# Sixteen start addresses for the split FFN weights of a two-layer decoder trunk

## The chip, the cores and the metric

The kernel runs on one core of one Trainium2 chip. The metric is the device time of one execution in microseconds; the kernel before takes 1004.91 us (median of 2 runs, 1004.67 to 1005.15).

## The reference

A trunk of two layers over one sequence of 256 tokens and 1024 features, in float32. Each layer has an FFN, an attention, and a second FFN, each ahead of it a root-mean-square norm that is scaled and shifted by vectors computed from `c`. So there are four FFNs:

```python
def swiglu(h, w_in, w_out):
    g, u = jnp.split(h @ w_in, 2, axis=-1)
    return (jax.nn.silu(g) * u) @ w_out
...
for layer in range(DEPTH):
    ...
    x = x + 0.5 * g1[:, None, :] * swiglu(h, ffn_w_in[layer, 0], ffn_w_out[layer, 0])
    ...
    x = x + g2[:, None, :] * mix
    h = modulate(rms_norm(x, norm_g[layer, 2]), sh3, sc3)
    x = x + 0.5 * g3[:, None, :] * swiglu(h, ffn_w_in[layer, 1], ffn_w_out[layer, 1])
return rms_norm(x, final_g)
```

The hidden width is 2816 (`FF`), so `w_in` is 1024 x 5632 and `w_out` is 2816 x 1024.

## The kernel before

Activations are kept transposed: 128 features on the partitions, the 256 tokens along each partition. A weight block of 128 x 128 is the stationary operand of a matmul (it is loaded into TensorE first, the profile's PEld), and 256 columns of activations are its moving operand. To keep float32 accuracy with a faster matmul type, every operand is split in two: a high part in the type fp32r and the rest, a low part. `mm3` (line 398) then makes three matmuls of each block: high weights by high activations, low weights by high activations, high weights by low activations. In the trace the weights' parts are `wh` and `wl`. The activations' parts are `HH` and `HL` (the normed input of a stage, rows of 320 words for each group of 128 features) in an FFN's first half of work, and `hidh` and `hidl` (the hidden units, tiles of 512 words) in its second.

All weights come in one fixed order, `stream`, cut in pieces of at most 1024 words per partition (`pieces`). For each piece there is a DMA from HBM into a buffer `raw`, a cast by ScalarE into a buffer `wh` (`cp_part`, line 288), and a subtraction by VectorE into a buffer `wl` (`sub_part`, line 298). There are 6 buffers `raw`, 6 `wh` and 5 `wl`, used in turn.

A buffer `wh` or `wl` is `WB` = 1088 words long, 64 more than a piece. 1088 words are 4352 bytes, or 17 x 256, so all eleven buffers start at the same address mod 256, which is 64 in the built program. `HH`, `HL`, `hidh` and `hidl`, and every block of 256 columns in them, start at 0 mod 256. So the distance "activations less weights, mod 256" is 192 for every such matmul. A dictionary `shift` moves the start of a piece's `wh` and `wl` inside its buffer by so many words. Before, it holds 16 words (64 bytes, distance 128) for six pieces: one at the second group of `win` of the FFN (0, 1), two at the first group of (1, 0), three at the second group of (1, 1):

```python
for (l, i), j, count in ((0, 1), 1, 1), ((1, 0), 0, 2), ((1, 1), 1, 3):
    first = next(...)
    shift.update({first + p: 16 for p in range(count)})
...
wh = wp.tile([P, WB], F32R, tag="wh", name="wh")[:, shift.get(u, 0):]
wl = wp.tile([P, WB], F32R, tag="wl", name="wl", bufs=NLO)[:, shift.get(u, 0):]
```

An FFN (`ffn(l, i, ...)`, line 532) has two stages. In the first, eleven groups of 256 hidden units are made from `win`: tiles `pg` and `pu`, 96 matmuls of 256 columns for a group, 24 for each piece of 1024 words. In the FFN (0, 0) the first four groups come from an own array `win0` (tiles `pf`) and seven from `win`. In (0, 1) and (1, 1) the first group is made ahead of the norm, with two further columns, so that its matmuls have 258 columns (tiles `lg`, `lu`). In the second stage, eight blocks of 128 output features are made from `wout` (tiles `po`), 66 matmuls each. Between the FFNs (0, 0) and (0, 1) stands the first attention (`wqk`, `wv`, `wo`; tiles `pqk`, `pv`, `pw`), between (0, 1) and (1, 0) the shared keys and values (`wkk`, `wkv`; tiles `lp`, `pk`, `pzf`, `pv`), between (1, 0) and (1, 1) the second attention.

The order on each engine is that in which the program is written. A small planner (`InOrder`, `bg`, `fill_act`, `fill_dve`) decides while the program is built where casts, subtractions and the dot products for `c` (`ada`) stand between the rest; its costs know sizes of operands, not addresses. Every instruction is issued through line 103, so the rows of the profile all name L103 and are told apart by their tiles.

Of the kernel before, what the change touches and what calls it, by code (L numbers as in the profile page):

```python
# [25 lines left out]
NG = FF // 256  # L26
# [5 lines left out]
K0 = 4  # L32
# [10 lines left out]
FRONT = 0  # L43
TAIL = 4
PLAN = [1, 1, 1, 1, 2, 1, 2, 3, 1, 3]
PACE = [0.62, 0.74, 0.62, 0.38, 0.76, 0, 0.74]
NRAW = 6
NLO = 5
# [59 lines left out]
def trunk(ctx, tc, a, out):  # L108
# [127 lines left out]
    def win0_of(l, i):  # L236
        return 0 if (l, i) == (0, 0) else 2 * (NG - K0) + 2 * NG * (2 * l + i - 1)

    def add_ffn(l, i):
        if (l, i) == (0, 0):  # L240
# [18 lines left out]
    pieces = [(src, c0, min(step, ncols - c0), c0 + step >= ncols)  # L259
              for src, ncols, step in stream for c0 in range(0, ncols, step)]  # L260

    shift = {}
    for (l, i), j, count in ((0, 1), 1, 1), ((1, 0), 0, 2), ((1, 1), 1, 3):
        first = next(p for p, v in enumerate(pieces) if v[0].tensor is a["win"].tensor
                     and v[0].offset == a["win"][win0_of(l, i) + 2 * j].offset)
        shift.update({first + p: 16 for p in range(count)})
    raws, his, los = [], [], []
    taken = [0]
    begun = [0]
# [228 lines left out]
    def late_pairs(src, dsts, m, then):  # L498

        pb = []

        def out(i):
            c = late_cols(pb[i])
            for b in range(2):
                t = kp.tile([P, S], F32, tag="sq", name="lt")
                dve.tensor_tensor(t, pb[i][b][:, :S], r, op=ALU.mult)
                act.activation(dsts[i][:, b * S:(b + 1) * S], t, AF.Identity, bias=c[:, b:b + 1])

        for i in range(2):
            banks = [mmbank(f"lp{i}{b}") for b in range(2)]
            pb.append(banks)
            blk = take(src)
            for k in range(NC):
                for b in range(2):
                    mm3(banks[b][:, :SX], blk(k * 256 + b * P), hx[k], k == 0, k == NC - 1)
                if i == 0:
                    if k == 2:
                        r = rstd_of(then)  # L520
                        mh = MakeH(r, m)
                else:
                    if k == 0:
                        out(0)
                    mh.go()
        mh.go(9 - mh.k)
        out(1)
        mode[0] = "run"
        return r
# [292 lines left out]

    pace[0] = PACE[0]
    ffn(0, 0, rstd, ((0, 1), (0, 0)), ((0, 4), (0, 3)))
# [173 lines left out]

    pace[0] = PACE[1]
    op = attention_a()  # L1000
    op.finish((0, 5), ((0, 7), (0, 6)))
    pace[0] = PACE[2]
    ffn(0, 1, "late", ((0, 7), (0, 6)), (("kv", 1), ("kv", 0)), at=3)
# [9 lines left out]
    for i in range(2):  # L1013
# [7 lines left out]
        fgs += [(fgh[:, k], fgl[:, k]) for k in range(4)]  # L1021
    pace[0] = PACE[3]
    rstd = late_pairs("wkk", kT, (("kv", 1), ("kv", 0)), AF.Exp)
# [46 lines left out]

    pace[0] = PACE[4]
    ffn(1, 0, "ready", None, ((1, 4), (1, 3)))

    def attention_b():
# [88 lines left out]
        def step(n):  # L1163
            for _ in range(n):
                next(fill, None)

        step(FRONT)
        for t in range(BH + 3):
            n0, n1 = PLAN[2 * (t // 4):2 * (t // 4) + 2]
            step(n0)  # L1170
# [15 lines left out]

    pace[0] = PACE[5]
    op = attention_b()
# [134 lines left out]
```

## Time and profile before

| | |
|---|---|
| median of 2 runs | 1004.91 us |
| the profiled execution, its own time | 1006.43 us |
| its span, first to last instruction | 1004.7 us |
| TensorE busy (matmuls) | 979.0 us, 97% |
| TensorE weight loads | 941.3 us, 94% |
| VectorE busy | 820.9 us, 82% |
| ScalarE busy | 563.3 us, 56% |
| mean granted TensorE clock | 0.997 |

The span is the time from the first to the last instruction of the program; the profiled execution's own time is 1.7 us longer. Matmuls overlap in a pipeline, so a matmul that is shown with 276 ns doesn't cost 276 ns: what it costs is the time from its start to the next one's start.

### The profile page before, as it was taken

What the parts mean: (1) busy time and instruction counts of PE and PEld (TensorE: products, weight loads), DVE (VectorE), ACT (ScalarE), POOL (GpSimd) and SP (SyncE); (2) the same over time, 40 slices, a digit from 0 to 9 for tenths busy, and PEclk for the clock granted to TensorE, in tenths of its full rate; (3) what the DMA queues carried; (4) which work ended last, traced back from release to release, by engine and by line L of the source; (5) the groups of instructions that cost most, each with busy time, mean ns of one, the idle gap of its engine ahead of it and who ended that gap; (6) DMA issues with size and microseconds to landing.
All of it is one profiled execution on the core that took longest, in us unless ns stands there. A gap on an engine that the chain in (4) does not pass through costs nothing.

```text
span 1004.7 us, 20432 instructions
## 1 busy us (share of the span) xinstructions
PE 979.0 (97%) x8076; PEld 941.3 (94%) x8076; DVE 820.9 (82%) x1379; ACT 563.3 (56%) x922; POOL 37.1 (4%) x64
## 2 busy tenths in 40 slices
PE   5999999999999999999999999999999999999996
PEld 4999999988989999999988999999987799999996
DVE  6989979889889998888698988889897787555553
ACT  5465545575877645455476455454575576454552
POOL 0000100000111000000000000000011010000000
PEclk9999999999999999999999999999999999999998
DMA  8988999958765899888757999989744337665661
GB/s 347 414 333 285 334 364 345 348 199 320 264 211 196 272 403 356 288 283 308 275 191 304 363 339 327 331 296 336 245 147 122 107 125 236 198 193 153 172 183 43
DMA packets 68131, 265.08 MB, mean 264 GB/s; under 512 B 7961, under 2 KB 8113, under 8 KB 57922
## 3 DMA queue, kind: packets, MB, share of 16 engines
q1 hardware_dynamic: 65810, 258.31, 73.3%
q0 software_dynamic: 1792, 4.81, 1.8%
q8 instruction: 63, 1.03, 0.4%
q10 hardware_dynamic: 432, 0.64, 0.2%
q14 instruction: 34, 0.28, 0.1%
HBM read 262.66 MB, written 2.65 MB: 264 GB/s over the span
## 4 chain that ended last, share of the span: by engine, by line
PE 92%; DVE 3%; ACT 2%; issue 1%; DMA 1%; SPq 0%; POOL 0%; DVEq 0%; POOLq 0%; ACTq 0%
PE po L103 24%; PE pg L103 21%; PE pu L103 21%; PE pf L103 5%; PE pv L103 4%; PE pw L103 4%; PE lp L103 2%; PE pqk L103 2%; PE pk L103 1%; PE pob L103 1%; PE lg L103 1%; PE lu L103 1%; PE sb L103 1%; DVE wl L103 1%; DMA ada<-in_ada 1%
## 5 line engine op out<-in xcount | busy, mean ns | idle before, releaser
L103 DVE TENSOR_TENSOR wl<-raw,wh 128x1024 fp32r<-128x1024 f32 (+1 forms) x368 | 401.3, 1104 | 92.8 <-issue 24.7
L103 ACT CAST wh<-raw 128x1024 fp32r<-128x1024 f32 (+1 forms) x368 | 349.3, 958 | 208.7 <-PE pu L103 96.5
L103 DVE CUSTOM_DVE_ANT_0 ada<-ada,cact,vecs 128x1024 f32<-128x1024 f32 x160 | 203.3, 1278 | 0.0
L103 PE MATMUL po<-hidl,wh 128*128 128x256 f32 x704 | 194.3, 276 | 0.0
L103 PE MATMUL po<-hidh,wh 128*128 128x256 f32 x704 | 194.3, 276 | 0.0
L103 PE MATMUL po<-hidh,wl 128*128 128x256 f32 x704 | 194.3, 276 | 0.0
L103 PE MATMUL pg<-HH,wh 128*128 128x256 f32 x608 | 168.1, 276 | 0.0
L103 PE MATMUL pg<-HH,wl 128*128 128x256 f32 x608 | 168.0, 276 | 0.0
L103 PE MATMUL pg<-HL,wh 128*128 128x256 f32 x608 | 168.0, 276 | 0.0
L103 PE MATMUL pu<-HH,wl 128*128 128x256 f32 x608 | 167.9, 276 | 0.0
L103 PE MATMUL pu<-HH,wh 128*128 128x256 f32 x608 | 167.9, 276 | 0.0
L103 PE MATMUL pu<-HL,wh 128*128 128x256 f32 x608 | 167.9, 276 | 0.0
L103 PEld LDWEIGHTS po<-hidh,wh 128*128 128x128 f32 x704 | 132.2, 188 | 0.0
L103 PEld LDWEIGHTS po<-hidh,wl 128*128 128x128 f32 x704 | 132.2, 188 | 0.0
L103 PEld LDWEIGHTS po<-hidl,wh 128*128 128x128 f32 x704 | 132.2, 188 | 0.0
L103 PEld LDWEIGHTS pg<-HH,wh 128*128 128x128 f32 x608 | 114.2, 188 | 0.7 <-issue 0.6
L103 PEld LDWEIGHTS pg<-HH,wl 128*128 128x128 f32 x608 | 114.2, 188 | 0.0
L103 PEld LDWEIGHTS pu<-HL,wh 128*128 128x128 f32 x608 | 114.2, 188 | 0.0
L103 PEld LDWEIGHTS pu<-HH,wl 128*128 128x128 f32 x608 | 114.1, 188 | 0.0
L103 PEld LDWEIGHTS pg<-HL,wh 128*128 128x128 f32 x608 | 114.1, 188 | 0.0
L103 PEld LDWEIGHTS pu<-HH,wh 128*128 128x128 f32 x608 | 114.1, 188 | 0.0
L103 ACT ACTIVATE HH<-ht,modall 128x256 fp32r<-128x256 f32 x56 | 27.8, 507 | 40.4 <-DVE ht L103 38.9
(204 smaller groups left out, 1604.7 us busy)
## 6 DMA issues: line engine op xcount, KB each, us to landing
raw<-in_win SPq DMA_DIRECT2D x176, 512.0 KB, 5.9
ada<-in_ada SPq DMA_DIRECT2D x79, 1024.0 KB, 7.4
raw<-in_wout SPq DMA_DIRECT2D x64, 384.0 KB, 4.9
raw<-in_wout SPq DMA_DIRECT2D x64, 320.0 KB, 4.3
raw<-in_wqk SPq DMA_DIRECT2D x16, 512.0 KB, 5.0
raw<-in_wo SPq DMA_DIRECT2D x16, 512.0 KB, 5.2
raw<-in_wv SPq DMA_DIRECT2D x8, 512.0 KB, 7.4
raw<-in_wkk SPq DMA_DIRECT2D x8, 512.0 KB, 8.1
```

The source lines that it names most:

```text
L103: return self.tc.keep_in_program_order(f(*args, **kw))
```

## The change

The dictionary `shift` is filled by another rule. A table `PHASES` gives a distance for each of sixteen halves of a stage: eight for `win` (two halves for each FFN, in the FFNs' order) and eight for `wout`. Every piece of `win` and of `wout` gets its start moved so that the distance from the activations has that value mod 256. The 16-word shifts of the six pieces are gone. `win0` and the weights of the attentions and of the shared keys and values keep the distance 192.

```diff
+PHASES = dict(win=(208, 224, 32, 48, 112, 144, 200, 184), wout=(240, 16, 80, 96, 160, 176, 168, 216))
...
     shift = {}
-    for (l, i), j, count in ((0, 1), 1, 1), ((1, 0), 0, 2), ((1, 1), 1, 3):
-        first = next(p for p, v in enumerate(pieces) if v[0].tensor is a["win"].tensor
-                     and v[0].offset == a["win"][win0_of(l, i) + 2 * j].offset)
-        shift.update({first + p: 16 for p in range(count)})
+    for name, at in PHASES.items():
+        ps = [p for p, v in enumerate(pieces) if v[0].tensor is a[name].tensor]
+        for p in ps:
+            u = (pieces[p][0].offset - a[name].offset) // math.prod(a[name].shape[1:])
+            if name == "wout":
+                q = divmod(u, 8)[0]
+            else:
+                f = 0 if u < win0_of(0, 1) else 1 + (u - win0_of(0, 1)) // (2 * NG)
+                b = win0_of(f // 2, f % 2)
+                q = 2 * f + (u - b >= (NG - K0 if f == 0 else NG))
+            shift[p] = (192 - at[q]) % 256 // 4
```

In the order of the program, with the number of matmuls by half:

| FFN | `win`, first and second half | `wout`, first and second half |
|---|---|---|
| (0, 0) | 208 (336), 224 (336) | 240 (264), 16 (264) |
| (0, 1) | 32 (96 of 258 columns, 432), 48 (528) | 80 (264), 96 (264) |
| (1, 0) | 112 (528), 144 (528) | 160 (264), 176 (264) |
| (1, 1) | 200 (96 of 258 columns, 432), 184 (528) | 168 (264), 216 (264) |

No instruction is added, taken away or moved: on every engine the same operations on the same tiles stand in the same order. What differs is the start of `wh` and `wl` inside their buffers.

## The prediction

> **What bounds the kernel now.** The page comes first: the engines' busy time, the clock, and the chain that ended last.
>
> ```profile
> span 1004.7 us, 20432 instructions
> PE 979.0 (97%) x8076; PEld 941.3 (94%) x8076; DVE 820.9 (82%) x1379; ACT 563.3 (56%) x922; POOL 37.1 (4%) x64
> PEclk9999999999999999999999999999999999999998
> PE 92%; DVE 3%; ACT 2%; issue 1%; DMA 1%; SPq 0%; POOL 0%; DVEq 0%; POOLq 0%; ACTq 0%
> ```
>
> TensorE is busy throughout at the full clock, and 92% of the chain is its own matmuls. The other engines count only where they make it wait. So the question is what one matmul costs in the FFNs. A table of the busy time in chosen windows shows it: us, then for each engine its busy time and the number of instructions. The windows are the FFNs after the first: groups 1 to 10 of (0, 1), then `wout`; (1, 0); groups 1 to 10 of (1, 1).
>
> ```profile
> 323.80:432.70 108.90, 108.90 (x962) 108.90 (x962) 98.84 (x134) 56.36 (x72) 0.00 (x0) 1.00 0.88 314
> 432.70:492.70 60.00, 60.00 (x530) 59.80 (x528) 51.14 (x80) 32.41 (x48) 1.93 (x4) 1.00 0.90 315
> 547.20:667.20 120.00, 120.00 (x1058) 119.96 (x1057) 106.32 (x141) 59.34 (x70) 0.00 (x0) 1.00 0.91 326
> 825.40:934.60 109.20, 109.20 (x962) 109.20 (x961) 66.12 (x74) 56.13 (x71) 0.00 (x0) 1.00 0.60 186
> ```
>
> TensorE never stops there: 960 matmuls in 108.9 us are 113.4 ns each, 528 in 60.0 us are 113.6 (the counts take in two that overlap the edges). Nothing in these stages waits for VectorE, ScalarE or a DMA; VectorE is nearly full in the first three (98.84 of 108.90) and half idle in the last, and the cost of a matmul is the same. What ends last is the beat of load and matmul itself.
>
> **What the beat depends on.** The change touches nothing but addresses, so I looked for stretches that run without a stop at another beat. Five windows: the three pieces at distance 128 (72 matmuls by the code); the piece-sized stretch behind them at 192 (72); `pzf`, whose weights start at 0 mod 256 (distance 0, 24 matmuls); the group `pk3` at 192 (48); and `lg`/`lu` at 192 with 258 columns (39).
>
> ```profile
> 825.44:833.98 8.54, 8.54 (x74) 8.54 (x73) 8.20 (x15) 6.36 (x14) 0.00 (x0) 1.00 0.43 123
> 835.36:843.52 8.16, 8.16 (x74) 8.16 (x73) 7.47 (x9) 5.64 (x7) 0.00 (x0) 1.00 0.77 244
> 514.71:517.59 2.88, 2.88 (x27) 2.88 (x26) 2.43 (x4) 2.88 (x5) 0.00 (x0) 1.00 0.15 51
> 517.58:523.24 5.66, 5.66 (x50) 5.66 (x49) 5.66 (x7) 5.57 (x9) 0.00 (x0) 1.00 0.81 250
> 319.05:323.76 4.71, 4.71 (x42) 4.71 (x40) 4.35 (x11) 3.16 (x6) 0.00 (x0) 1.00 0.65 226
> ```
>
> Divided by the matmuls that start in them: 118.6 ns at distance 128, 113.3 at 192, 120.0 at 0, 117.9 at 192 in `pk3`, and 120.8 with 258 columns. Two facts follow. The distance bears on the beat: where it goes from 128 back to 192 in the middle of group 1 of (0, 1), with nothing else changed, the starts in order of time close up within three matmuls.
>
> ```profile
> 325.90 0.28 PE L103 MATMUL pu<-HH,wh 128*128 128x256 f32 x1
> 326.02 0.28 PE L103 MATMUL pu<-HH,wl 128*128 128x256 f32 x1
> 326.14 0.28 PE L103 MATMUL pu<-HL,wh 128*128 128x256 f32 x1
> 326.25 0.28 PE L103 MATMUL pu<-HH,wh 128*128 128x256 f32 x1
> ...
> 326.95 0.28 PE L103 MATMUL pg<-HH,wh 128*128 128x256 f32 x1
> 327.07 0.28 PE L103 MATMUL pg<-HH,wl 128*128 128x256 f32 x1
> 327.18 0.28 PE L103 MATMUL pg<-HL,wh 128*128 128x256 f32 x1
> 327.29 0.28 PE L103 MATMUL pu<-HH,wh 128*128 128x256 f32 x1
> ```
>
> Four starts before the seam span 0.35 us, four behind it 0.34. And the distance alone doesn't settle it: `pk3` runs at 117.9 at the good distance. So at 192 there are two steady ways to run, a good beat and one off it, and the one in which a stage starts it keeps.
>
> **The good beat is the floor.** A row for each kind of matmul gives the shortest, the middle and the longest duration; off the beat they are longer (the second pair: `pk` off the beat, `pzf`).
>
> ```profile
> L103 PE MATMUL po<-hidh,wh x704: 276/276/276, 139.9 to 994.1; 128*128 128x256 f32 x176
> L103 PE MATMUL pg<-HH,wh x608: 276/276/385, 62.8 to 933.6; 128*128 128x256 f32 x152
> ...
> L103 PE MATMUL pk<-HL,wh 128*128 128x256 f32 x16 | 4.5, 281 | 0.0
> ...
> L103 PE MATMUL pzf<-HH,fgh 128*128 128x256 f32 x8 | 2.3, 283 | 0.0
> ```
>
> The middle one is the shortest one: of the 1312 in the first two rows, at distances 192 and 128 and after every kind of disturbance, none is shorter than one on the good beat. What speaks for a lower floor are matmuls of another type (float32, 128 columns), which take less:
>
> ```profile
> L103 PE MATMUL po<-va,wt x48: 271/275/275, 245.5 to 298.2; 128*128 128x128 f32 x48
> L103 PE MATMUL po<-tri,on x16: 272/272/273, 253.8 to 303.0; 128*128 128x128 f32 x16
> ```
>
> [...]
>
> **The change part by part.** (1) *Taken away:* the six pieces at distance 128. 6 x 24 = 144 matmuls at 118.6 - 113.3 = 5.3 ns over the floor: at most 0.8 us to gain. The 192 matmuls of 258 columns (`lg`, `lu`) are 7.5 ns over it; at 32 and 200 they could gain up to 1.4 us or lose nothing that I can price, and I take 0. So the most that the floor leaves is 2.2 us.
>
> (2) *Added:* new distances for 2 x 336 + 6 x 528 + 8 x 264 = 5952 matmuls, 5760 without those of 258 columns. Off the beat each costs 4.6 ns (`pk3`) to 6.7 (`pzf`) more; I take 5.3, as at 128, which is the case nearest to a weight piece that starts elsewhere in an FFN. All 5760 off it: 5760 x 5.3 = 30.5 us, by the ends 26.5 to 38.6. None: 0.
>
> How many? No run here shows any of the sixteen. Of the three distances that the trace has, 192 can hold the beat and 0 and 128 don't, in 24 and 144 matmuls. Six halves' distances lie within 24 bytes of 192 (168, 176, 184, 200, 208, 216): 336 + 432 + 528 + 3 x 264 = 2088 matmuls. For them I take the nearest row, 192, with one way of two: half off the beat, 1044. The other ten (3672 matmuls) lie nearer to 0, to 128, or to 64, of which no row of an FFN tells: I take the count of three, two thirds off, 2448. Together 3492 x 5.3 = 18.5 us.
>
> (3) *The writers.* ScalarE and VectorE write at other starts. The row for 1024 words with a shift of 64 bytes, and the one behind it without:
>
> ```profile
> L103 DVE TENSOR_TENSOR wl<-raw,wh 128x1024 fp32r<-128x1024 f32 x4 | 4.9, 1217 | 0.0
> ...
> L103 DVE TENSOR_TENSOR wl<-raw,wh 128x1024 fp32r<-128x1024 f32 x5 | 5.9, 1216 | 0.0
> ```
>
> 1 ns. A start 8 bytes off a multiple of 16 (168, 184, 200, 216) isn't shown. What hides a slower write is VectorE's idle time: in 547.20:667.20, 13.7 us over 44 pieces, some 0.3 us for each write of 1.2; above a quarter more it would come on the path. I take 0. The DMAs land in `raw`, whose addresses stay.
>
> (4) *Seams.* Fifteen changes of distance without a stop, three matmuls each by the starts above: under 0.3 us.
>
> Sum: 18.5 - 0.8 = +17.7 us, against a profiled execution of 1006.43 us (span 1004.7). That execution lies 0.15% over the median of the runs, so I add the difference to the median: 1004.9 + 17.7 = 1022.6, say **1022 us**.
>
> [...]
>
> **The rivals.** *A, the forecast:* some halves keep the beat, some don't, 1009 to 1030. Chance 0.58.
>
> *B, not slower:* the good beat, once entered, holds at every distance but a few, as it holds at 192 through each seam from `pg` to `po`, where tiles and strides change and the beat doesn't; (0, 0) enters it from `pf` at 192, and every later half takes it over. Its place are the seams, its price 0, its gain 0.8 us: 1004.1. It decides if 0 and 128 are special, as multiples of 128. Against it: three stages at 128 in a row never fell into the beat. Chance 0.14, with what lies up to 1009.
>
> *C, nearly all lose it:* the beat needs a start on a multiple of 64, as every operand that the trace shows has, and none of the sixteen is one; a row of weights then costs what two columns more cost the 258-column matmuls, 7.5 ns. 5952 x 7.5 - 0.8 = +43.8: 1049; with 5.3 ns, 1035. For it: no odd start holds the beat anywhere; against: none is tried. Chance 0.24.
>
> *D, faster:* one distance or more lowers the floor to what the float32 rows hint at, 1 to 4 ns less: at most 5760 x 4 = 23 us, if all did. The 276 in thousands speak against it. Chance 0.04.
>
> That the change doesn't do what it says isn't a rival: in the built program each of the 5952 has its distance.
>
> **How the numbers follow.** The forecast is A's. The range goes from B's 1004 to 1040, most of C; D and C's top, under 0.15 together, are left out. A measurement of this kernel can tell about 2% from no change, 20 us. Slower by more than that is C and the part of A above 1025: 0.24 + 0.18 = 0.42. Faster by more needs D at nearly its full size: 0.02. The rest, 0.56, is within.
>
> **What would show it.** In the new trace, windows over each half: 113.3 ns for each matmul where the beat holds, with durations of 276 ns, and 117 to 121 with 281 or more where not. (1) shows in the first groups of (0, 1), (1, 0), (1, 1); (3) in the durations of `wl<-raw,wh`. The attentions should keep their times but for which of their two ways they start in, some 4.6 ns on each of about 900 matmuls, 4 us at most. I would be wrong if a half ran under 113, if a lost beat cost 10 ns or more, or if VectorE made TensorE wait.

## The result, and the profile after

The changed kernel takes 1033.47 us (median of 2 runs, 1032.82 to 1034.12) against 1004.91: a recorded ratio of 1.0272, 95% interval 1.0246 to 1.0298 (the two medians alone give 1.0284). It is 28.6 us slower. The profiled execution took 1032.82 us, its span is 1031.0.

The page, the same lines as before; the kernel is eight lines longer, so the helper's line is L104 now:

```profile
span 1031.0 us, 20432 instructions
PE 1007.7 (98%) x8076; PEld 970.0 (94%) x8076; DVE 822.9 (80%) x1379; ACT 563.7 (55%) x922; POOL 37.0 (4%) x64
PEclk9999999999999999999999999999999999999998
PE 90%; DVE 4%; ACT 3%; DMA 1%; issue 1%; POOL 0%; SPq 0%; DVEq 0%; ACTq 0%; POOLq 0%
```

The number of instructions is the same (20432), the granted clock is the same (0.997), and TensorE is busy for 28.7 us more (1007.7 against 979.0). Next the busy time in windows over the sixteen halves, in the order of the program. The first row is `pf`, whose distance of 192 didn't change. Of the second half of `win` of (0, 0) only the 264 matmuls behind a stop are shown, and of the first halves of (0, 1) and (1, 1) the 432 matmuls of 256 columns.

```profile
14.62:63.16 48.54, 48.53 (x385) 48.12 (x385) 47.16 (x72) 24.78 (x30) 0.00 (x0) 1.00 1.02 415
63.16:102.92 39.76, 39.76 (x339) 39.76 (x337) 31.67 (x40) 21.34 (x26) 0.00 (x0) 1.00 0.75 255
112.26:143.61 31.35, 31.35 (x266) 31.35 (x265) 25.97 (x41) 14.01 (x18) 4.72 (x9) 1.00 0.98 362
143.61:174.84 31.23, 31.23 (x266) 31.23 (x265) 26.79 (x42) 16.74 (x25) 0.00 (x0) 1.00 0.89 322
174.84:205.82 30.98, 30.98 (x267) 30.98 (x265) 25.90 (x41) 16.95 (x25) 0.00 (x0) 1.00 0.95 346
329.66:380.55 50.89, 50.89 (x435) 50.89 (x434) 50.36 (x73) 28.25 (x39) 0.00 (x0) 1.00 0.86 313
380.55:442.15 61.60, 61.60 (x531) 61.60 (x530) 49.09 (x62) 28.15 (x33) 0.00 (x0) 1.00 0.87 297
442.15:473.32 31.17, 31.17 (x266) 31.17 (x265) 26.17 (x40) 16.78 (x25) 0.00 (x0) 1.00 0.87 302
473.32:505.00 31.68, 31.68 (x266) 31.63 (x264) 26.13 (x41) 16.62 (x24) 1.92 (x4) 1.00 0.92 312
558.37:621.73 63.36, 63.36 (x529) 63.36 (x528) 55.80 (x75) 30.87 (x37) 0.00 (x0) 1.00 0.89 309
621.73:685.09 63.36, 63.36 (x531) 63.36 (x530) 50.76 (x67) 28.14 (x33) 0.00 (x0) 1.00 0.88 306
685.09:716.41 31.32, 31.32 (x266) 31.32 (x265) 28.36 (x44) 16.64 (x25) 0.00 (x0) 1.00 0.87 307
716.41:747.74 31.33, 31.33 (x266) 31.33 (x265) 26.35 (x43) 16.75 (x25) 0.82 (x2) 1.00 0.78 254
846.09:896.98 50.89, 50.89 (x435) 50.89 (x434) 34.53 (x42) 27.69 (x38) 0.00 (x0) 1.00 0.59 198
896.98:959.46 62.48, 62.48 (x531) 62.48 (x530) 31.64 (x32) 28.44 (x33) 0.00 (x0) 1.00 0.53 165
959.46:989.39 29.93, 29.93 (x266) 29.93 (x265) 17.37 (x23) 16.82 (x25) 0.00 (x0) 1.00 0.65 188
989.39:1020.85 31.46, 31.46 (x266) 31.46 (x265) 13.81 (x20) 11.97 (x19) 0.00 (x0) 1.00 0.28 82
```

Divide each window by its matmuls (336, 264, 264, 264; 432, 528, 264, 264; 528, 528, 264, 264; 432, 528, 264, 264), as in the prediction: 118.3 ns at 208, 118.8 at 224 (one stop of 0.1 us in it), 118.3 at 240, 117.3 at 16; 117.8 at 32, 116.7 at 48, 118.1 at 80, 120.0 at 96; 120.0 at 112, 120.0 at 144, 118.6 at 160, 118.7 at 176; 117.8 at 200, 118.3 at 184, **113.4 at 168**, 119.2 at 216. One half of sixteen keeps the beat. Of the sixteen windows TensorE stops only in that of 224; VectorE is half idle in the last ones (busy 31.64 of 62.48 us at 184) and the price is no lower (118.3).

The rows of the durations (shortest, middle, longest) say it in short: in `po` and `pg` the middle one has left the shortest one. The last row is `pf` in the kernel before.

```profile
L104 PE MATMUL po<-hidh,wh x704: 276/281/286, 143.6 to 1020.5; 128*128 128x256 f32 x176
L104 PE MATMUL pg<-HH,wh x608: 276/281/385, 63.2 to 958.4; 128*128 128x256 f32 x152
L104 PE MATMUL pf<-HH,wh x128: 281/281/581, 14.6 to 62.8; 128*128 128x256 f32 x128
...
L103 PE MATMUL pf<-HH,wh x128: 276/276/582, 15.8 to 62.4; 128*128 128x256 f32 x128
```

The third row is a surprise: `pf` was on the beat before (276) and is off it now, with nothing in it changed. All of it is off, so its middle duration is its shortest one all the same; only the comparison with 276 shows it.

### The profile page after: what moved, and what is told of

It reads as the page before. It is cut to its first block, busy times and chain, and to the rows that moved or that the text cites. A ratio compares the mean times of both kernels' runs of the same rounds, so it can differ in the third digit from the quotient of the medians.

```text
span 1031.0 us, 20432 instructions
## 1 busy us (share of the span) xinstructions
PE 1007.7 (98%) x8076; PEld 970.0 (94%) x8076; DVE 822.9 (80%) x1379; ACT 563.7 (55%) x922; POOL 37.0 (4%) x64
## 4 chain that ended last, share of the span: by engine, by line
PE 90%; DVE 4%; ACT 3%; DMA 1%; issue 1%; POOL 0%; SPq 0%; DVEq 0%; ACTq 0%; POOLq 0%
PE po L104 23%; PE pg L104 21%; PE pu L104 21%; PE pf L104 5%; PE pv L104 4%; PE pw L104 4%; PE lp L104 2%; PE pqk L104 1%; PE pk L104 1%; PE pob L104 1%; PE lg L104 1%; PE lu L104 1%; DVE wl L104 1%; PE sb L104 1%; DMA raw<-in_wkk 1%
## 5 line engine op out<-in xcount | busy, mean ns | idle before, releaser
L104 DVE TENSOR_TENSOR wl<-raw,wh 128x1024 fp32r<-128x1024 f32 (+1 forms) x368 | 402.9, 1105 | 115.6 <-issue 33.8
L104 ACT CAST wh<-raw 128x1024 fp32r<-128x1024 f32 (+1 forms) x368 | 348.8, 955 | 237.0 <-PE pu L104 110.2
L104 DVE CUSTOM_DVE_ANT_0 ada<-ada,cact,vecs 128x1024 f32<-128x1024 f32 x160 | 203.3, 1278 | 0.0
L104 PE MATMUL po<-hidh,wh 128*128 128x256 f32 x704 | 197.3, 280 | 0.0
L104 PE MATMUL po<-hidh,wl 128*128 128x256 f32 x704 | 197.2, 280 | 0.0
L104 PE MATMUL po<-hidl,wh 128*128 128x256 f32 x704 | 197.1, 280 | 0.0
L104 PE MATMUL pu<-HH,wh 128*128 128x256 f32 x608 | 171.4, 282 | 0.0
L104 PE MATMUL pg<-HH,wl 128*128 128x256 f32 x608 | 171.0, 281 | 0.0
L104 PE MATMUL pg<-HH,wh 128*128 128x256 f32 x608 | 171.0, 281 | 0.0
L104 PE MATMUL pg<-HL,wh 128*128 128x256 f32 x608 | 170.9, 281 | 0.0
L104 PE MATMUL pu<-HH,wl 128*128 128x256 f32 x608 | 170.8, 281 | 0.0
L104 PE MATMUL pu<-HL,wh 128*128 128x256 f32 x608 | 170.7, 281 | 0.0
L104 PEld LDWEIGHTS po<-hidl,wh 128*128 128x128 f32 x704 | 132.6, 188 | 0.0
L104 PEld LDWEIGHTS po<-hidh,wl 128*128 128x128 f32 x704 | 132.3, 188 | 0.0
L104 PEld LDWEIGHTS po<-hidh,wh 128*128 128x128 f32 x704 | 132.3, 188 | 0.0
L104 PEld LDWEIGHTS pg<-HH,wh 128*128 128x128 f32 x608 | 114.6, 189 | 0.7 <-issue 0.6
L104 PEld LDWEIGHTS pg<-HH,wl 128*128 128x128 f32 x608 | 114.8, 189 | 0.0
L104 PEld LDWEIGHTS pu<-HH,wl 128*128 128x128 f32 x608 | 114.8, 189 | 0.0
L104 PEld LDWEIGHTS pu<-HL,wh 128*128 128x128 f32 x608 | 114.7, 189 | 0.0
L104 PEld LDWEIGHTS pu<-HH,wh 128*128 128x128 f32 x608 | 114.7, 189 | 0.0
L104 PEld LDWEIGHTS pg<-HL,wh 128*128 128x128 f32 x608 | 114.6, 189 | 0.0
L104 ACT ACTIVATE HH<-ht,modall 128x256 fp32r<-128x256 f32 x56 | 27.8, 507 | 39.8 <-DVE ht L104 38.0
```

Of the source, the lines that this page charges most:

```text
L104: return self.tc.keep_in_program_order(f(*args, **kw))
```

## The experiments

Two theories. **D**: each distance has its own steady price, and few have a way at 113.3 ns. **E**: any distance can run either way, and a stage keeps the way in which it starts. Each price is the time from start to start in the run's own trace. Where a time stands without a ratio it is that of a single run, so the argument there rests on the windows. Ratios are the recorded ones, which differ a little from the quotient of the medians.

**All at 192, no shifted pieces.** The table, and nothing else of the change's kernel, is edited:

```diff
-PHASES = dict(win=(208, 224, 32, 48, 112, 144, 200, 184), wout=(240, 16, 80, 96, 160, 176, 168, 216))
+PHASES = dict(win=(192,) * 8, wout=(192,) * 8)
```

> All FFN weight pieces at distance 192, the six shifted pieces of before taken away. Theory D (the distance decides: a steady beat of 113.3 ns exists at few distances, 192 among them, and a stage falls into it by itself): every FFN half at 113.3 ns a matmul, 1004.1 us, 0.8 under before. Theory E (entry decides: at any distance there is a good and a bad way to run, a stage keeps the one it starts in, and the shifted pieces were what put three stages into the good one): the stages of (0,1), (1,0) and (1,1) at 117.8 ns, up to 4572 matmuls x 4.5 ns = +20 us, 1024 us.

1024.39 us against 1007.84 for the kernel before beside it, ratio 1.0137 (1.0088 to 1.0186). Windows: `wout` of (0, 0), then `win` of (0, 1), (1, 0) and (1, 1):

```profile
139.05:198.89 59.84, 59.84 (x530) 59.84 (x529) 53.70 (x84) 34.48 (x51) 0.00 (x0) 1.00 0.94 347
322.95:436.02 113.07, 113.07 (x963) 113.07 (x961) 99.43 (x134) 56.30 (x72) 0.00 (x0) 1.00 0.83 304
552.51:676.89 124.38, 124.38 (x1058) 124.37 (x1057) 106.55 (x141) 59.18 (x70) 0.00 (x0) 1.00 0.90 315
837.52:950.59 113.07, 113.07 (x962) 113.07 (x961) 66.08 (x74) 55.92 (x71) 0.00 (x0) 1.00 0.56 180
```

113.3 ns in the first FFN, 117.8 in the three that follow a stop or the 258-column matmuls. So at 192 theory E holds: two ways, 113.3 and 117.8, and each of these stages keeps its own. The six shifted pieces, which I priced as 0.8 us to save, were worth 16.5 us between these medians.

**All at 168.**

```diff
+PHASES = dict(win=(168,) * 8, wout=(168,) * 8)
```

> All FFN weight pieces of win and wout at distance 168, the only one of the sixteen that ran at 113.3 ns. Theory D: 168 has a steady beat that is entered from any state, so all sixteen halves at 113.3 ns, 1003 to 1005 us. Theory E: 168 was entered by luck from the half before it; some halves at 117 to 120, 1010 to 1030 us.

1004.52 us against 1007.84, ratio 0.9962 (0.9944 to 0.9979). The end of `pf`, `win` of (0, 0) up to its stop, then `win` of (0, 1):

```profile
56.40:61.70 5.30, 5.30 (x46) 5.30 (x46) 4.17 (x5) 4.64 (x6) 0.00 (x0) 1.00 1.02 411
61.70:109.39 47.69, 47.69 (x410) 47.56 (x408) 41.32 (x53) 28.43 (x35) 0.00 (x0) 1.00 0.80 278
324.04:432.88 108.84, 108.84 (x963) 108.84 (x961) 98.95 (x135) 56.25 (x72) 0.00 (x0) 1.00 0.87 314
```

113.4 ns (960 matmuls) in (0, 1), and on the beat without shifted pieces in (1, 0) and (1, 1) as well, but 116.9 (408) in the first FFN. So 168 has a second way too, a cheaper one, and fell into it once. The trace shows where from: a stop in `pf` at 55.9 us had thrown `pf` off the beat (its last 45 matmuls at 117.8), 168 was entered from there without a stop, and the stop at 109 us brought it onto the beat (`wout` behind it takes 59.84 us for 528, 113.3). So here one stop threw a stage off, to 117.8, and another put one right, from 116.9.

**The same sixteen, five halves later.**

```diff
+PHASES = dict(win=(176, 200, 216, 208, 16, 32, 96, 112), wout=(184, 168, 224, 240, 48, 80, 144, 160))
```

> The same sixteen distances, each five halves later in the program (the last five come first). Theory D: the distance decides, so again only the half at 168 (now the second half of wout of the first FFN) at 113.3 ns, and the others near the ns that they had in the change (112, 144, 96 near 120; 16, 32, 48 near 117); 1031 to 1036 us. Theory E: other halves fall on the beat, and 168 need not; no distance keeps its ns.

1033.45 us. The halves at 168, 208, 32 and 112:

```profile
173.47:203.40 29.93, 29.93 (x266) 29.93 (x265) 25.91 (x41) 16.87 (x25) 0.00 (x0) 1.00 0.94 334
379.14:441.62 62.48, 62.48 (x530) 62.48 (x529) 48.66 (x61) 28.21 (x33) 0.00 (x0) 1.00 0.84 286
621.38:682.98 61.60, 61.60 (x530) 61.60 (x529) 50.74 (x67) 28.14 (x33) 0.00 (x0) 1.00 0.90 314
895.15:958.51 63.36, 63.36 (x531) 63.36 (x530) 31.63 (x32) 28.43 (x33) 0.00 (x0) 1.00 0.52 162
```

113.4 at 168 in another stage of another FFN, 118.3 at 208 and 120.0 at 112 as before; 16 (not shown) and 32 have changed their price (117.3 to 120.0, 117.8 to 116.7) but not found the beat. Here 168, 208 and 112 kept their price in another place, and the beat went with the distance.

**Entered from the beat.** The kernel before, with its shifted pieces, and four distances in `wout` alone:

```diff
+WOUT = (208, 192, 176, 192, 184, 192, 200, 192)
+    for p, v in enumerate(pieces):
+        if v[0].tensor is a["wout"].tensor:
+            u = (v[0].offset - a["wout"].offset) // math.prod(a["wout"].shape[1:])
+            shift[p] = (192 - WOUT[u // 8]) % 256 // 4
```

> The kernel before with its shifted pieces; only the first half of each wout stage gets another distance (208, 176, 184, 200 in the four FFNs), entered without a stop from win at 192 on the beat; the second half is at 192 again. Theory D: these four have no steady beat, so 118 to 119 ns at once though entered from the beat (4 x 264 x 5 ns = +5.3 us, 1010 us), and 192 takes the beat up again behind them. Theory E: entered from the beat they keep it: 113.3 ns, 1005 us.

1010.78 us; the kernel before beside it took 1007.84. The last stage, 200 and then 192:

```profile
937.81:968.90 31.09, 31.09 (x267) 31.09 (x265) 17.37 (x23) 16.85 (x25) 0.00 (x0) 1.00 0.63 183
968.90:998.82 29.92, 29.92 (x266) 29.92 (x265) 13.80 (x20) 11.96 (x19) 0.00 (x0) 1.00 0.30 85
```

117.8 ns at once, though entered from 113.3; and 113.3 again at 192. 208, 176 and 184 took 117.8, 118.8 and 118.3, and 192 took the beat up behind each. These distances have no way on the beat that a start from it finds: theory D for them.

**The other multiples of 8, and sixteen odd multiples of 4.**

```diff
+PHASES = dict(win=(8, 24, 72, 88, 136, 152, 0, 64), wout=(40, 56, 104, 120, 232, 248, 128, 168))
```

> The change with another sixteen distances, in the order of the program 8, 24, 40, 56, 72, 88, 104, 120, 136, 152, 232, 248, 0, 64, 128, 168: with the change's own, every multiple of 8. Theory D (each distance has its own steady price; only few have a way at 113.3 ns): 168 at 113.3 again, now as the last half, 0 and 128 at 118.5 to 120, and most others 116 to 120; 1030 to 1036 us. If the good distances form a band (168 and 192 its edges were ruled out by 176 and 184), none of the new ones holds. Theory N (chance decides in which way a half runs): a third of the halves at 113.3 and 168 not among them for sure; near 1020 us.

```diff
+PHASES = dict(win=(164, 172, 188, 196, 4, 36, 132, 220), wout=(156, 180, 204, 148, 68, 100, 236, 212))
```

> Sixteen distances that are odd multiples of 4, in the order of the program 164, 172, 156, 180, 188, 196, 204, 148, 4, 36, 68, 100, 132, 220, 236, 212. Theory D: prices as smooth as between 8-byte steps: those next to 168 (164, 172) and to 192 (188, 196) may hold the beat, the others 116 to 120; 1025 to 1036 us. If starts must lie on 8 bytes, all sixteen lose more than any before, over 121 ns: over 1045 us.

1027.84 and 1036.24 us, the first under the 1030 that I expected, because 64 and 88 hold the beat. Windows of the first sweep at 88, 64 and 168:

```profile
380.46:440.32 59.86, 59.86 (x531) 59.86 (x529) 48.88 (x62) 28.15 (x33) 0.00 (x0) 1.00 0.88 308
894.79:954.63 59.84, 59.84 (x530) 59.84 (x529) 31.64 (x32) 28.44 (x33) 0.00 (x0) 1.00 0.55 171
985.95:1015.90 29.95, 29.95 (x267) 29.95 (x266) 13.82 (x20) 11.96 (x19) 0.00 (x0) 1.00 0.30 85
```

and of the second at 180 and 204:

```profile
174.96:204.92 29.96, 29.96 (x267) 29.96 (x266) 25.89 (x41) 16.86 (x25) 0.00 (x0) 1.00 0.91 329
443.02:472.98 29.96, 29.96 (x267) 29.96 (x265) 25.97 (x40) 16.63 (x25) 0.00 (x0) 1.00 0.89 309
```

113.4, 113.3, 113.4, then 113.5 and 113.5. The good ones stand 12 bytes apart, 168, 180, 192, 204, and in mirrored pairs: 64 is 256 - 192, 88 is 256 - 168. All others lie between 115.6 (248) and 120.7 (36), but for 72 matmuls at 24 that took 123.3. So the band that I imagined around 192 has teeth: 172, 176, 184, 188, 196, 200 are all off the beat (176, 184 and 200 at 118.7, 118.3 and 117.8 in the change's trace).

**Mirrors.** Only distances found or mirrored:

```diff
+PHASES = dict(win=(64, 64, 88, 88, 180, 180, 204, 204), wout=(76, 52, 204, 180, 64, 88, 52, 76))
```

> Only distances that the two sweeps found or that mirror them: win 64, 88, 180, 204 in the four FFNs, wout 76, 52, then 204, 180, then 64, 88, then 52, 76; no shifted pieces. 168, 180, 192, 204 held 113.3 ns in the sweeps, and so did 64 and 88, which are 256 less 192 and less 168. Theory M (the good distances stand in mirrored pairs d and 256 - d): 52 and 76, which no run had, hold 113.3 as well, and every wout half is on the beat. Against it: 52 and 76 at 116 to 120. The starts of win behind a stop show which distance a stage enters by itself; if all do, 1003 to 1005 us, and each win stage that doesn't costs 3 to 7 ns for 960 to 1056 matmuls, 3 to 7 us.

1019.11 us; the kernel before beside it took 1011.58 in its one run. `wout` of (0, 0) at 76 and 52, `win` of (0, 1) at 88, of (1, 0) at 180, and `wout` of (1, 1) at 52 and 76:

```profile
142.94:174.14 31.20, 31.20 (x267) 31.20 (x265) 27.45 (x43) 17.46 (x26) 0.00 (x0) 1.00 0.92 326
174.14:206.70 32.56, 32.56 (x267) 32.56 (x266) 26.26 (x41) 17.04 (x25) 0.00 (x0) 1.00 0.92 330
330.63:445.83 115.20, 115.20 (x962) 115.20 (x961) 99.58 (x134) 56.44 (x72) 0.00 (x0) 1.00 0.84 299
560.62:680.31 119.69, 119.69 (x1058) 119.69 (x1056) 106.34 (x141) 59.06 (x70) 0.00 (x0) 1.00 0.91 326
947.29:977.21 29.92, 29.92 (x267) 29.92 (x266) 17.38 (x23) 16.80 (x25) 0.00 (x0) 1.00 0.65 190
977.21:1007.14 29.93, 29.93 (x267) 29.93 (x266) 13.82 (x20) 11.94 (x19) 0.00 (x0) 1.00 0.30 86
```

Entered from 204 on the beat, 52 and 76 hold it (113.3, 113.4): the mirror is right. Entered off it, the same two take 123.3 (52) and 118.2 (76), and 88, which had held it, takes 120.0 for 960 matmuls. So the low four have second ways that a stage stays in, though not after every bad stretch: in the first sweep 88 and 64 found the beat behind 72 (117.8) and 0 (120.0). 180 (once behind a stop) and 204 found it each time (113.3 to 113.5). Neither theory holds alone: few distances have a way at 113.3 ns, as D says, and at six of the eight found a stage can also keep another, as E says.

**Which of the two addresses?** First the distance 168 made by moving the activations by 232 bytes, then starts moved by 64:

```diff
+O = 58
-    hx = [(HH[:, k, :SX], HL[:, k, :SX]) for k in range(NC)]
-    hn = [(HH[:, k, :S], HL[:, k, :S]) for k in range(NC)]
+    hx = [(HH[:, k, O:O + SX], HL[:, k, O:O + SX]) for k in range(NC)]
+    hn = [(HH[:, k, O:O + S], HL[:, k, O:O + S]) for k in range(NC)]
...
+PHASES = dict(win=(192,) * 8, wout=(168,) * 8)
```

> The distance 168 made from the other side: the weights of win start at 64 mod 256 as at distance 192, and the normed activations HH and HL start 58 words (232 bytes) later in their rows, so that activations less weights is 168 for win, win0 and the projections from HH; wout at 168 by its weights. No shifted pieces. Theory of the distance: the win halves of (0,1), (1,0) and (1,1) run at 113.3 ns as with the weights moved, 1003 to 1006 us. Theory of the weights' own start (64 mod 256 gave 117.8 without the shifted pieces): these halves at 117.8, 2976 matmuls x 4.5 ns = +13 us, 1018 us.

1032.42 us. `win` of (0, 1), and `wout` of (1, 0):

```profile
329.95:445.15 115.20, 115.20 (x963) 115.20 (x962) 99.60 (x135) 56.55 (x72) 0.00 (x0) 1.00 0.84 298
687.12:747.00 59.88, 59.88 (x531) 59.88 (x530) 54.43 (x86) 33.33 (x50) 0.81 (x2) 1.00 0.84 286
```

Neither theory: 120.0 ns in `win`, where I expected 113.3 or 117.8; `wout` at 168 from hidden tiles at 0 holds the beat. Moved by 64 bytes instead (the table counts from activations at 0, so it holds the weights' starts):

```diff
+O = 16
+PHASES = dict(win=(128, 0, 0, 128, 192, 64, 104, 168), wout=(168,) * 8)
```

> HH and HL start 16 words (64 bytes) later in their rows, a multiple of 64 as before; wout stays at 168 from hidden tiles that start at 0. The win halves have, in the order of the program, weights starting at 128, 0; 0, 128; 64, 192; 152, 88 mod 256, so distances 192, 64; 64, 192; 0, 128; 168, 232. Theory of the distance: 113.3 ns in the halves with 192, 64 and 168 (those behind a stop may lie in their second way, 116 to 118), and 118 to 120 in those with 0, 128 and 232. Theory of the weights' own start (64, 192, 88 good whatever the activations' start, 0, 128 and 152 not): the opposite halves, 113.3 with starts 64, 192 and 88.

1017.97 us. Halves of `win` with weights at 128, 64, 192, 152 and 88:

```profile
376.22:436.07 59.85, 59.85 (x531) 59.85 (x529) 48.81 (x62) 28.14 (x33) 0.00 (x0) 1.00 0.88 308
550.26:613.61 63.35, 63.35 (x530) 63.35 (x528) 55.94 (x75) 31.03 (x37) 0.00 (x0) 1.00 0.88 310
613.61:676.26 62.65, 62.65 (x531) 62.65 (x529) 50.74 (x67) 28.13 (x33) 0.00 (x0) 1.00 0.90 312
834.50:883.50 49.00, 49.00 (x434) 49.00 (x433) 34.54 (x43) 27.66 (x38) 0.00 (x0) 1.00 0.62 204
883.50:946.16 62.66, 62.66 (x531) 62.66 (x529) 31.64 (x32) 28.46 (x33) 0.00 (x0) 1.00 0.52 165
```

113.4 at distance 192, 120.0 at 0, 118.7 at 128, 113.4 (432 matmuls) at 168, 118.7 at 232: the prices that these distances have elsewhere, while the weights' own starts say the opposite. At 64 (not shown) the 72 matmuls ahead of the stop in (0, 0) held 113.3, and behind that stop and the next 64 lay in its second way, at 117.8. So it is the distance, with activations that start 0 or 64 bytes past a multiple of 256; at 232 bytes past, the good distance 168 cost 120.0. Other starts, 16 bytes for one, weren't tried.

**All weights at 168**, `win0`, the attentions and the shared keys and values too:

```diff
+    shift = {p: 6 for p in range(len(pieces))}
```

> Every weight piece, those of win0, of the attentions and of the shared keys and values too, at distance 168. Theory D with 168 entered from most starts: the matmuls of 256 columns in pqk, pw, pk and pq run at 113.3 where half of them were at 117.8 (864 x 0.5 x 4.5 ns = -1.9 us against all FFN pieces at 168), the 258-column ones stay near 120: 1002 to 1004 us against 1004.5 for that kernel. If a stop throws 168 off as it does 192: the same time as that kernel.

1010.99 us against 1005.49, ratio 1.0048 (1.0033 to 1.0064), slower than either theory had it. In the profiled run, the slowest of seven at 1018.37 us, both stages of (0, 0) and of (1, 0) lie in 168's second way at 116.7; `win` of (1, 0):

```profile
554.46:677.66 123.20, 123.20 (x1058) 123.19 (x1056) 106.44 (x139) 59.16 (x69) 0.00 (x0) 1.00 0.90 316
```

**All FFN pieces at 180, and at 204**, `win0` too:

```diff
+PHASES = dict(win=(180,) * 8, wout=(180,) * 8)
+    shift.update({p: (192 - 180) % 256 // 4 for p, v in enumerate(pieces) if v[0].tensor is a["win0"].tensor})
```

> All FFN weight pieces, win0 too, at distance 180, no shifted pieces. 180 was at 113.3 ns in each of the three stretches that had it, one of them entered off the beat and one behind a stop. Theory: it has no second way that the stages fall into, so every FFN stage at 113.3 ns in every run, 1003 to 1004.5 us, and runs that differ less than those of the kernel before. Rival: it has a second way too, which 1056 + 528 matmuls did not show; a stage in it costs 3 to 7 ns a matmul, 1007 to 1025 us.

> The same at distance 204, which was at 113.3 ns in each of the three stretches that had it, two of them entered off the beat. Theory and rival as for 180: 1003 to 1004.5 us in every run, or 1007 to 1025 us where a stage falls into a second way.

1004.40 us (12 runs, 1003.3 to 1005.2) and 1004.74 (12 runs, 1003.5 to 1006.2), against 1005.59 for the kernel before (23 runs, 1005.0 to 1013.7): ratios 0.9987 (0.9978 to 0.9995) and 0.9977 (0.9961 to 0.9994). Every FFN stage of both profiled runs is on the beat (`win` of (0, 1) and (1, 1) takes 108.8 us for 960 in both, 113.3); `win` of (1, 0) at 180:

```profile
545.96:665.64 119.68, 119.68 (x1057) 119.68 (x1056) 106.38 (x141) 59.03 (x70) 0.00 (x0) 1.00 0.92 325
```

113.3 ns. By the ratios both lie 0.1 to 0.2% under the kernel before, the same time at 2%, and their runs differ less. Both are close to the 1003 to 1004.5 us that I expected of every run, and none comes near the rival's 1007. That they beat the kernel with `win` and `wout` at 168 isn't shown: that one took 1004.52 us, at a ratio of 0.9962, in another set of runs.

## Why the prediction was right or wrong

The direction, the bound and the range were right; the size was short, +17.7 of +28.6 us. The stretch of rival A, 1009 to 1030 us, ended below the result, and the greatest chance, 0.56, stood on a change of under 2%; slower by more had 0.42.

- *The beat bounds the FFNs, and 113.3 ns is its floor.* Right: no half in any of the runs went under it, and rival D fell.
- *The price off the beat, 5.3 ns.* Right in the mean: the windows after lie 28.2 us over 113.3 ns a matmul, with the 72 matmuls not shown 28.5, which is 5.2 for each of the 5496 off the beat. It isn't one price: 3.3 at 48, 6.7 at 96, 112 and 144.
- *How many lose it.* This step failed. I took half of the near six and two thirds of the others, 3492 matmuls; it was 5496. Of the 2004 missing, 780 are near ones (1824 lost it, not 1044) and 1224 belong to the other ten, which all lost it (3672, not 2448). Nearness to 192 says nothing, since good distances stand on isolated points, and only 168 of the six is one; and the count of three (192, 0 and 128) was too few to tell how rare they are. At the measured price the 2004 matmuls are 10.4 us, and 17.7 + 10.4 = 28.1.
- *The shifted pieces, 0.8 us to gain.* Right for this kernel, whose halves lose the beat anyway, and wrong as a reading of them: all at 192 shows that without them three FFNs run at 117.8.
- *The writers and the seams at nothing.* Right: the one seam onto the beat, into 168, leaves its 264 matmuls at 29.93 us, 0.01 over 264 x 113.33 ns, and the mean subtraction of 1024 words is 1220 ns in both profiles, before and after.

```profile
L103 DVE TENSOR_TENSOR wl<-raw,wh 128x1024 fp32r<-128x1024 f32 x240 | 289.5, 1220 | 52.8 <-issue 19.4 <-PE pu L103 14.6 <-ACT sg L103 12.0
L104 DVE TENSOR_TENSOR wl<-raw,wh 128x1024 fp32r<-128x1024 f32 x240 | 290.2, 1220 | 66.0 <-issue 26.1 <-ACT sg L104 17.7 <-PE pu L104 14.7
```

- *Rival B, the beat once entered holds:* wrong. 208, 176, 184 and 200 lost it at once when entered from it (117.8, 118.8, 118.3, 117.8).
- *Rival C, nearly all lose it:* the time was its, at its lower price (1035), and its reason was wrong. 180 and 204 aren't multiples of 64, nor even of 8, and hold the beat (113.3 to 113.5).
- *A start off a multiple of 16*, for which (3) had no row, didn't by itself cost the weights the beat: 168 puts them 8 bytes past such a multiple and 180 puts them 12 past, both at 113.3 to 113.5 ns.

What the prediction didn't have: `pf` fell off the beat in this run, 356 of its 384 matmuls at 117.8 instead of 113.4 ns from start to start (most of the others, its first, start 0.21 us apart in both kernels), 1.6 us. 28.5 - 0.8 + 1.6 is 29.3 against 26.3 between the two spans; 1.1 of the rest is that `pf` starts earlier (at 14.62 instead of 15.75 us), 1.0 is a wait in front of `lp` behind (0, 1) that shrank from 1.2 to 0.2 us, and 0.9 I haven't traced.

Open is what in the chip makes these eight distances good. The runs show the pattern, not the circuit.

## What to carry to other kernels

Where TensorE runs without a stop, look at the time from start to start, and compare it and the durations with those of the best stretch of the same kind (113.3 and 276 ns here). That the middle duration is the shortest one isn't enough, as `pf` at 281/281 shows. If a stretch is slower, the addresses of its two operands may be what costs: 3 to 6% here, in most cases (116.7 to 120.0 against 113.3 ns), without one more instruction. Here a good stretch at one address difference didn't make its neighbours good (180 at 113.3, 176 and 184 at 118.7 and 118.3), and one good stretch didn't make a difference safe (88 at 113.4, then at 120.0): try it behind a stop and from a bad stretch. Take the difference that gets back by itself, as 180 and 204 did here, rather than one that needs a push, as 192 did.

## What the runs showed of the hardware

With activations that start at 0 mod 256 (64, 168 and 192 were also tried with starts at 64), pairs of a 128-column load and a 256-column fp32r matmul ran at 113.3 ns at the distances 52, 64, 76, 88, 168, 180, 192 and 204 mod 256, and at none of the other 42 tried (115.6 to 123.3 ns; all multiples of 8 and eighteen odd multiples of 4 were). This doesn't rule out more good ones: only twelve of the 42 were entered straight from the beat (0 in the kernel before's `pzf`; 8, 104, 128, 148, 164, 176, 184, 200, 208, 216, 232), and 52, 76 and 88 missed it too when they were entered off it (123.3, 118.2 and 120.0).

Six of the eight showed a second steady way, at 116.7 (168), 117.8 (64, 192), 118.2 (76), 120.0 (88) and 123.3 ns (52); for 180 and 204 none was seen. Off the beat four distances showed two prices as well: 16 at 117.3 and 120.0, 32 at 117.8 and 116.7, 208 at 118.3 and 117.8, 24 at 123.3 in 72 matmuls and 120.7 or less in its others. In no profiled run did the FFN matmuls of 256 columns, once settled, change from one steady way to another except at a stop or another distance (the 1056 of `win` of (1, 0) stayed at 113.3 at 180, at 116.7 at 168 and at 117.8 at 192). `pf` at 192 starts in the second way in two of the nine profiled runs that have it there, the change's and the one with the mirrors (a middle duration of 281 ns, 276 in the other seven). This fits the kernel before's runs of up to 1013.7 us, though none of those was profiled.
